# Third and fourth Strassen sums in a buffer of their own, nine Strassen operand pairs, 205 Strassen steps at other places

## The chip, the cores and the metric

The kernel runs on one core of one Trainium2 chip. The metric is the device time of one execution in microseconds, the median of several runs. Beside it there is one profiled execution, whose trace gives what each engine did.

## The reference

A decoder block over 256 tokens of 4096 channels, in float32. Cut to what matters:

```python
h = rmsnorm(x, norm_w)
proj = einsum('bsd,de->bse', h, w_in)            # 4096 -> 20480
u_p, z_p, u_c, b_c, c_c, z_c, g_logit = split(proj)
y_pool = causal_multiscale_pool(u_p, pool_w[l], pool_scale) * silu(z_p)
y_conv = causal_gated_shortconv(u_c, b_c, c_c, conv_w, conv_b) * silu(z_c)
br = einsum('bsnc,ncd->bsnd', stack([y_pool, y_conv]), w_branch)   # 2 x (2048 -> 4096)
merged = sum(sigmoid(g_logit + gate_b) * br, axis=n)
x = x + einsum('bsd,de->bse', merged, w_out)     # 4096 -> 4096
return rmsnorm(x, final_norm_w)
```

## The kernel before

**Units and steps.** The three large products are cut into units of 1024 output columns: 20 of the input projection (cu, cc, cz, cb for the two halves of the convolution branch, pz and pu for the two halves of the pooling branch, then eight gate units g0_0, g1_0, ... g1_3), eight of the branch projection (b0_0, b1_0, ...), four of the output projection (o0 to o3). They run in the order given here. A unit sums over steps; one step brings 256 rows of the weights (two blocks of 128 rows by 1024 columns, 1 MB) and multiplies them with one *operand pair*, the matching 256 channels of all 256 tokens, which stay in SBUF in a tile named `arena`. A unit of the input or output projection has 16 steps, one for each operand pair; a branch unit has eight. In two units (pz1 and g0_0) three more steps, for the pooling, stand among the first.

**Precision.** Each float32 factor is cut into a high part (ScalarE copies it to the matmul type `F32R`) and a low part (VectorE subtracts the high part from the original), and a product is three matmuls: high by high, high by low, low by high.

**P steps and S steps.** A plain step (P) is 2 token halves x 2 column halves x 2 row blocks x 3 = 24 matmuls of 128x512. A Strassen step (S) takes seven block products for eight, 7 x 3 = 21 matmuls, and pays for it in sums: of the operand pair once (the blocks called Q3, Q5, Q6, Q7 in the arena), and of the weights in every S step. `Step.micros` lists what a step prepares. For a P step these are two halves, each with a copy by ScalarE and a subtraction by VectorE of 128x1024. For an S step: `sums` adds the first two sums, 128x1024, into `V`; `direct` copies and subtracts three raw blocks (128x1536), and adds the third and the fourth sum (128x512 each) into `raw` itself, over blocks 0 and 1; `t13` splits V; `t24` splits the third and fourth sum. All results go to `ring`, a ring buffer of 60 pieces of 1 KB per partition. A P step takes 16 pieces, an S step 28.

**What sets the order.** Every engine runs its instructions in program order, and the order is written by the planner at build time. `pump` issues the next weight load (SyncE's queue, three `raw` buffers of 1 MB) once the step three before is *prepared*, and prepares a step up to AHEAD = 3 steps before its matmuls, as soon as the ring has room. `tick` runs once in every 6 matmuls: it takes the next item of `queue` (a unit's epilogue: its joins, sigmoid, products, transposes, stores) and advances the filling of the operand pairs of the next projection (`pop_fill`: a sum set and a split). The large adds between units and the transfers of intermediate results are issued on GpSimd's queue.

**Operand pairs.** Of the 16 pairs NP_X = 9 have plain slots and NS_X = 7 have Strassen slots. An S step needs a pair with a Strassen slot; a P step can use either kind. One of the seven slots (NB = 1) has two blocks more, so that its plain and its Strassen form stand side by side. Because some units have eight S steps, one plain pair (`LATE`) gets its sums separately: `late_sums` makes them at step 23 and stores them in DRAM, `early_place` and `late_split` fetch and split them for later units, and `late_m` does the same in o1. The sums of the other pairs are made by `x_sums` and split by `x_parts` at the steps that `seconds` lists.

**Which steps are S steps.** Each unit has a sequence of P and S, made by `spread_sequence`, `late_sequence`, `at_places` and the table `SPREAD`. In all there are 188 S steps and 260 P steps.

Of the kernel before, what the change touches and what calls it, by code (L numbers as in the profile page):

```python
# [42 lines left out]
NP_X, NS_X = 9, 7  # L43
NB = 1
NP_Y, NS_Y = (6, 5), (2, 3)
RING = 60
# [10 lines left out]
def hybrid_block(ctx: ExitStack, tc: tile.TileContext, x, x_t, norm_t, w_first, w_in, pool_w, pool_scale,  # L57
# [52 lines left out]
    V = sb("V", [P, 2, NH])  # L110
    cnt = sb("cnt", [P, 2])
# [16 lines left out]
    late_d = dram.tile([P, 5, P], F32, name="late_d")  # L128
# [62 lines left out]
    class Operand:  # L191


        def __init__(self, kind, view, region):
            self.kind, self.view, self.region = kind, view, region
            self.ready = False
            self.more = None
            self.more_ready = False

        def block(self, part, i):  # L200

            if self.kind == "S":
                return self.view[:, part, i]
            if i in self.more:
                return self.more[i][:, part]
            return self.view[:, part, {A12: 0, A22: 0, A11: 1, A21: 1}[i], i in (A22, A21)]
# [40 lines left out]
    class Step:  # L247
# [7 lines left out]
        def micros(self):  # L255
# [30 lines left out]
            if self.kind == "S":  # L286
                q = r.rearrange("p (i n) -> p i n", i=4)
                tv = V

                def sums(_):  # L290
                    add(tv, q[:, 0:1].to_broadcast([P, 2, NH]), q[:, 1:3])

                def direct(block):
                    self.bd = block
                    d = piece(block, 0, 12).rearrange("p (i a n) -> p i a n", i=3, a=2)
                    self.dh, self.dl = d[:, :, 0], d[:, :, 1]
                    act(self.dh, q[:, 1:4])
                    add(q[:, 0], tv[:, 0], q[:, 2])
                    sub(self.dl, q[:, 1:4], self.dh.bitcast(F32))
                    add(q[:, 1], q[:, 0], q[:, 3])  # L300

                def t13(block):
                    self.b13 = block
                    t = piece(block, 0, 8).rearrange("p (i a n) -> p i a n", i=2, a=2)
                    self.h13, self.l13 = t[:, :, 0], t[:, :, 1]
                    act(self.h13, tv)
                    sub(self.l13, tv, self.h13.bitcast(F32))
# [297 lines left out]
    SPREAD = {"cc1":(8,1),"cb1":(8,2),"cu1":{4,5,7,9,10,12,13,15},"cb0":(8,2),"cz0":(7,5),"pz0":{5,7,8,10,11,13,15},"pu0":(7,),"cz1":(7,5),"g1_3":(6,0),"pz1":(7,),"g0_0":(7,),"pu1":{4,6,8,10,12,13,15},"cc0":{2,4,6,8,10,13,15}}  # L605
# [26 lines left out]
    def in_unit(name, col, epi, seq=None, **kw):  # L632
        def src(i):
            return win[col // NU, i]
        if name in SPREAD:
            at = SPREAD[name]
            seq = at_places(at) if isinstance(at, set) else spread_sequence(*at)
# [5 lines left out]
        units.append(Unit(name, src, seq or seq_late, x_ops, epi, scaled=True, **kw))  # L643
        return units[-1]


    def conv_units(c, first=False):
# [32 lines left out]
        in_unit(f"cu{c}", base, lambda u: [], seq=seq_0 if first else spread_sequence(NS_X, 4), dst=Y)  # L680
        in_unit(f"cc{c}", base + 2 * HALF, c_epi, seq=seq_even if c else None)
        in_unit(f"cz{c}", base + 3 * HALF, z_epi)
        in_unit(f"cb{c}", base + HALF, b_epi, seq=seq_even)


    def pool_units(c):
        def z_epi(u):
            return sigmoid_mul() + [
                lambda: move(E[:, 0], pool_scale[0, None, c * NU:(c + 1) * NU].to_broadcast([P, NU]))
            ] + gap(5) + [lambda: mul(Y, R, E[:, 0:1].to_broadcast([P, 2, NU]))]  # L690

        in_unit(f"pz{c}", HALF + c * NU, z_epi, seq=None if c else seq_turned)
        in_unit(f"pu{c}", c * NU, lambda u: [])
        return units[-1]


    def make_bands(c):
        nonlocal sa, Y
        if c == 0:
            x_ops[LATE].more_ready = False  # L700

# [78 lines left out]
    def gate_unit(n, c, before=None):  # L780
# [7 lines left out]
        seq = {(0, 0): seq_late, (1, 3): spread_sequence(few)}.get((n, c), seq_even)  # L788
        if (n, c) in ((0,1),(1,1),(0,2),(1,2),(0,3),(1,0),):
            seq = spread_sequence(NS_X + 1, 1 if c else 2)  # L790
# [27 lines left out]

    def out_unit(c):
# [14 lines left out]
        seq = seq_even if c else seq_late  # L834
        if c in (2,):
            seq = spread_sequence(NS_X + 1)
        if c == 1:
            seq = at_places({2,4,6,7,9,11,13,15})

            late_s = [i for k, i in seq if k == 'S']  # L840
            late_s = iter(late_s[1:] + late_s[:1])
            seq = [(k, next(late_s) if k == 'S' else i) for k, i in seq]
        if c == 3:

            seq = spread_sequence(NS_X, 1, TAIL + 0)
        if c == 2:
            seq = at_places({2,4,6,7,9,11,13,15})
# [133 lines left out]
    def insert(u, c, owner):  # L981
# [144 lines left out]
    LATE = NP_X - 1  # L1126

    def late_sums():
        o = x_ops[LATE]
        h, l = (o.view[:, part].bitcast(F32) for part in range(2))  # L1130
        q = sa[:, 4:8].rearrange("p (k t) c -> p k t c", t=2)
        add(q, h, l)
        q = q.rearrange("p k t c -> p k (t c)")
        mul(q, q, rbc[:, None].to_broadcast([P, 2, T]))
        sums_s(sa, [sa[:, i] for i in range(4, 8)])
        mul(sa[:, Q3], sa[:, Q3], std)
        move(late_d[:, 0:4], sa[:, 0:4])
        move(late_d[:, 4], sa[:, A11])

    def late_place(pool, o, blocks):  # L1140
        n = len(blocks)
        q = pool.tile([P, 2, n, P], F32R, name="sums")
        o.more = {b: q[:, :, i] for i, b in enumerate(blocks)}
        return q

    def late_split(o, place, src):

        q = []
        return [lambda: (q.append(place()), act(q[0][:, 0], src)),
                lambda: (sub(q[0][:, 1], src, q[0][:, 0].bitcast(F32)), setattr(o, "more_ready", True))]  # L1150

    early = []

    def early_place():

        pool = replace_by("early")
        src = pool.tile([P, 5, P], F32, name="early_src")
        move(src, late_d)
        early.extend(late_split(x_ops[LATE], lambda: late_place(pool, x_ops[LATE], (Q3, Q5, Q6, Q7, A11)), src))

    late = []

    def late_m():
        nonlocal Y
        pool = replace_by("late_m", lower)
        stages.pop()
        Y = pool.tile([P, 1, NU], F32, name="Y")
        sums_s(sa, [sa[:, i] for i in range(4, 8)])
        late.append(late_place(pool, m_ops[LATE], (Q3, Q5, Q6, Q7)))

# [12 lines left out]
    seconds = {14: 10, 15: 11, 16: 12, 17: 13, 19: 14, 21: 15, 28: 9}  # L1183
# [50 lines left out]
    def pump():  # L1234

        while True:
            moved = False
            nl = state["nl"]
            if nl < len(loaded) and (nl < NRAW or loaded[nl - NRAW].prepared):
# [7 lines left out]
            if i < len(steps) and i <= state["limit"]:  # L1247
                s = steps[i]
                if s.src is None or s.raw is not None:
# [10 lines left out]
                    if not state["micros"]:  # L1260
                        s.prepared = True
# [6 lines left out]
    for s in steps:  # L1268
        s.prepared = False
# [36 lines left out]
    def queue_fills():  # L1306
# [26 lines left out]
        for i in order_of(seq_late):  # L1333
            from_m(m_ops[i], i)

    def run_step(u, st):
# [14 lines left out]
        assert st.kind != "S" or st.op.kind == "S" or st.op.more_ready  # L1351
# [11 lines left out]
    for u in units:  # L1363
# [11 lines left out]
        for st in u.steps:  # L1375
# [11 lines left out]
            if u.name == "g0_0" and st is u.steps[2]:  # L1387
                move(sa[:, 0:5], late_d)
            if u.name == "g0_0" and st is u.steps[8]:
                queue.extend(late_split(x_ops[LATE], lambda: late_place(  # L1390
                    replace_by("late", lower), x_ops[LATE], (Q3, Q5, Q6, Q7, A11)), sa[:, 0:5]))
            if u.name == "o1" and st is u.steps[4]:
                assert not fills
                move(flat(sa[:, 4:8]), m_d[LATE // 4][:, LATE % 4].rearrange("p k t -> p (k t)"))
                queue.extend(gap(7) + [late_m] + late_split(m_ops[LATE], lambda: late[0], sa[:, 0:4]))
# [179 lines left out]
```

## Time and profile before

| | |
|---|---|
| median of 3 runs | 2378.28 us (2378.14 to 2378.44) |
| span of the profiled execution, first to last instruction | 2376.6 us |
| time of the runs outside that span | about 1.7 us |
| PE busy | 2364.3 us (99%), 10540 instructions |
| DVE busy | 2170.1 us (91%) |
| ACT busy | 1392.8 us (59%) |
| POOL busy | 86.0 us (4%) |
| HBM read and written | 516.60 MB and 25.49 MB |
| granted TensorE clock | 0.999 |

PE is TensorE, PEld its weight loads, DVE VectorE, ACT ScalarE, POOL GpSimd, SP SyncE. A line such as L1283 is a line of the kernel's file; most elementwise work goes through one helper, so that it has one line (L72 for VectorE's two-tensor operations, L69 for ScalarE) and is told apart by its tiles. In `ring<-raw,ring` the tile left of the arrow is written, those right of it are read. The records of matmuls overlap, so their mean (390 ns) is not their pace.

### The profile page before, as it was taken

How to read it: one execution, taken by the hardware profiler on the slowest of the kernel's cores; microseconds unless marked ns; L12 is line 12 of the kernel's file. 1: busy time of each engine (PE TensorE's matmuls, PEld its weight loads, DVE VectorE, ACT ScalarE, POOL GpSimd, SP SyncE). 2: the span in 40 equal slices, each digit the busy share in tenths (PEclk: the TensorE clock that was granted, in tenths of full speed). 3: DMA queues.
4: the chain of work that ended last, by engine and by line, in shares of the span. 5: the costliest groups of instructions: out<-in, count | busy, mean ns of one | idle time of the engine just before them, and what ended most of it. 6: DMA issues, size and time to landing. Idle time of an engine off the chain costs nothing.

```text
span 2376.6 us, 27878 instructions
## 1 busy us (share of the span) xinstructions
PE 2364.3 (99%) x10540; PEld 1957.5 (82%) x10540; DVE 2170.1 (91%) x2195; ACT 1392.8 (59%) x1452; POOL 86.0 (4%) x153
## 2 busy tenths in 40 slices
PE   9999999999999999999999999999999999999998
PEld 7888888888888888888888888888888888888886
DVE  8999999989989978979999999999898898799998
ACT  7565665656546555556655656556664556566554
POOL 0000000000010010000000000000100001000000
PEclk9999999999999999999999999999999999999999
DMA  8464665655665646655776667667766667567666
GB/s 337 161 238 170 235 251 211 217 211 213 212 239 217 238 183 221 231 200 201 259 247 214 235 237 235 228 238 260 263 249 230 226 250 289 209 214 265 241 240 264
DMA packets 83559, 551.25 MB, mean 232 GB/s; under 512 B 9616, under 2 KB 9872, under 8 KB 22240
## 3 DMA queue, kind: packets, MB, share of 16 engines
q1 hardware_dynamic: 68800, 484.51, 54.7%
q0 software_dynamic: 14192, 63.90, 9.6%
q8 instruction: 82, 1.34, 0.2%
q10 hardware_dynamic: 432, 1.07, 0.1%
q14 instruction: 53, 0.43, 0.1%
HBM read 516.60 MB, written 25.49 MB: 228 GB/s over the span
## 4 chain that ended last, share of the span: by engine, by line
PE 98%; DVE 1%; DMA 1%; ACT 0%; SPq 0%; issue 0%; DVEq 0%; ACTq 0%
PE sums L1283 74%; PE shared L1283 21%; PE shared L766 1%; PE shared L509 1%; DMA raw<-in_w_in_dram 0%; DVE R L72 0%; DVE ring L72 0%; DMA raw<-in_w_out_dram 0%; ACT ring L69 0%; PE shared L745 0%; SPq L87 0%; PE shared L746 0%; PE shared L748 0%; SPq L162 0%; ACT V L69 0%
## 5 line engine op out<-in xcount | busy, mean ns | idle before, releaser
L1283 PE MATMUL sums<-ring,arena 128*128 128x512 f32 x7890 | 1858.2, 390 | 0.5 <-ACT arena L69 0.4
L1283 PEld LDWEIGHTS sums<-ring,arena 128*128 128x128 f32 x7890 | 1478.3, 188 | 307.8 <-ACT ring L69 1.2
L69 ACT ACTIVATE ring<-raw 128x1024 fp32r<-128x1024 f32 (+2 forms) x902 | 997.5, 1145 | 703.9 <-DVE raw L72 297.3
L72 DVE TENSOR_TENSOR ring<-raw,ring 128x1024 fp32r<-128x1024 f32 (+2 forms) x902 | 1176.5, 1335 | 142.5 <-ACT ring L69 108.6
L1283 PE MATMUL shared<-ring,arena 128*128 128x512 f32 x2118 | 535.2, 389 | 0.0
L1283 PEld LDWEIGHTS shared<-ring,arena 128*128 128x128 f32 x2118 | 397.6, 188 | 82.5
L69 ACT ACTIVATE ring<-V 128x1024 fp32r<-128x1024 f32 x188 | 198.8, 1058 | 148.3 <-DVE V L72 112.7
L72 DVE TENSOR_TENSOR V<-raw 128x1024 f32<-128x1024 f32 x188 | 229.3, 1220 | 4.7 <-DMA raw<-in_w_in_dram 2.6
L72 DVE TENSOR_TENSOR ring<-V,ring 128x1024 fp32r<-128x1024 f32 x188 | 229.3, 1220 | 0.5 <-ACT ring L69 0.5
L72 DVE TENSOR_TENSOR raw<-raw 128x512 f32<-128x512 f32 x188 | 130.2, 693 | 6.5
L72 DVE TENSOR_TENSOR raw<-V,raw 128x512 f32<-128x512 f32 x188 | 130.0, 692 | 5.8
L72 DVE TENSOR_TENSOR R<-R,E 128x1024 f32<-128x1024 f32 (+1 forms) x49 | 77.5, 1591 | 1.6 <-ACT E L69 0.9
L72 DVE TENSOR_TENSOR R<-R,shared 128x512 f32<-128x512 f32 x87 | 59.5, 684 | 8.9 <-ACT R L69 5.0
L69 ACT ACTIVATE E<-sums,rin 128x512 f32<-128x512 f32 x76 | 50.0, 685 | 15.7 <-PE sums L1283 15.7
L69 ACT ACTIVATE arena<-sa 128x512 fp32r<-128x512 f32 (+2 forms) x42 | 22.4, 559 | 35.5 <-DVE sa L72 35.5
L1283 PE MATMUL shared<-ring,sums 128*128 128x512 f32 x138 | 35.9, 396 | 0.0
L1283 PEld LDWEIGHTS shared<-ring,sums 128*128 128x128 f32 x138 | 25.9, 188 | 6.0
L94 POOL DMA_DIRECT2D R<-E x8 | 7.2, 980 | 513.6 <-ACT ring L69 337.9
L69 ACT ACTIVATE E<-sums 128x512 f32<-128x512 f32 x40 | 22.2, 592 | 5.4 <-PE sums L1283 5.1
L72 DVE TENSOR_TENSOR arena<-sa,arena 128x512 fp32r<-128x512 f32 (+2 forms) x42 | 24.4, 606 | 0.7 <-ACT arena L69 0.7
L94 POOL DMA_DIRECT2D R<-in_gate_b_dram x9 | 10.1, 1119 | 356.0 <-DVE R L72 348.3
L509 PEld LDWEIGHTS shared<-ident,R 128*128 128x128 f32 x160 | 19.4, 140 | 4.2
(149 smaller groups left out, 515.8 us busy)
## 6 DMA issues: line engine op xcount, KB each, us to landing
raw<-in_w_in_dram SPq DMA_DIRECT2D x318, 1024.0 KB, 4.9
raw<-in_w_branch_dram SPq DMA_DIRECT2D x64, 1024.0 KB, 5.4
raw<-in_w_out_dram SPq DMA_DIRECT2D x64, 1024.0 KB, 5.0
gates_d<-R POOLq DMA_DIRECT2D x8, 1024.0 KB, 9.1
R<-in_gate_b_dram POOLq DMA_DIRECT2D x7, 1024.0 KB, 11.2
R<-E POOLq DMA_DIRECT2D x4, 1024.0 KB, 8.7
raw<-in_pool_w_dram SPq DMA_DIRECT2D x4, 1024.0 KB, 5.0
Y<-gates_d POOLq DMA_DIRECT2D x4, 1024.0 KB, 7.9
```

The costliest lines, as they stand in the source:

```text
L69: return pin(nc.scalar.activation(dst, src, func, **kw))
L72: return pin(nc.vector.tensor_tensor(out=dst, in0=a, in1=b, op=op))
L94: return pin(nc.gpsimd.dma_start(dst, src, accum_op=ALU.add))
L509: pin(nc.tensor.transpose(shared(j)[:, i * T + t * P:i * T + (t + 1) * P], src[:, t, c:c + P], ident))
L766: pin(nc.tensor.matmul(o, a[:, k, ts], b[:, k], start=(k, i) == (0, 0), stop=(k, i) == (3, 2)))
L1283: pin(nc.tensor.matmul(ps, lhs, rhs, start=n == 0, stop=n == u.total[b] - 1))
```

## The change

It does these things:

- A new tile `W` of the size of V takes the third and the fourth sum, which were written over the raw weights.
- A step has a second mark, `split`, set when `direct` is done (for a P step, when it is prepared). `pump` issues the load three steps on by that mark and no longer by `prepared`.
- Nine pairs have Strassen slots and seven have plain ones; two of the nine (NB = 2) have the two blocks more. The functions for the late pair are gone, with their DRAM tile and their transfers; `seconds` makes the sums of pairs 8 and 7 at steps 32 and 36.
- The order of P and S steps comes from a table of places for each unit, 205 S steps and 243 P steps in all. Units with nine S steps appear. `insert` puts several S steps between two P steps in pz1 and g0_0.
- The ring has 62 pieces. The scratch that is set aside for descriptors of GpSimd's transfers is set to 2048 bytes per partition.

```diff
-NP_X, NS_X = 9, 7
-NB = 1
+NP_X, NS_X = 7, 9
+NB = 2
...
-RING = 60
+RING = 62
...
+    W = sb("W", [P, 2, NH])
...
-                    add(q[:, 0], tv[:, 0], q[:, 2])
+                    add(W[:, 0], V[:, 0], q[:, 2])
                     sub(self.dl, q[:, 1:4], self.dh.bitcast(F32))
-                    add(q[:, 1], q[:, 0], q[:, 3])
+                    add(W[:, 1], W[:, 0], q[:, 3])
+                    self.split = True
...
-                    act(self.h24, q[:, 0:2])
-                    sub(self.l24, q[:, 0:2], self.h24.bitcast(F32))
+                    act(self.h24, W)
+                    sub(self.l24, W, self.h24.bitcast(F32))
...
+    PLACES = {
+        "cc0": (2, 4, 6, 7, 10, 12, 15),
+        "cz0": (5, 7, 8, 10, 11, 13, 15),
+        "cb0": (1, 3, 5, 6, 8, 11, 12, 14, 15),
+        "cu1": (4, 5, 7, 9, 10, 11, 12, 14, 15),
+        "cc1": (3, 5, 6, 8, 9, 11, 12, 14, 15),
...
+        "pz1": (3, 6, 8, 9, 10, 11, 12, 14, 15),
+        "pu1": (4, 5, 6, 9, 10, 12, 13, 15),
+        "g0_0": (3, 6, 8, 9, 10, 12, 14, 15),
+        "g1_0": (2, 4, 5, 7, 8, 9, 11, 13, 15),
+        "g0_1": (2, 4, 6, 7, 8, 10, 11, 13, 15),
...
+    }
...
+    OUT = ((6, 7, 9, 10, 11, 13, 15), (2, 4, 6, 7, 8, 10, 12, 13, 15), (2, 4, 6, 9, 11, 13, 15), (1, 3, 4, 7, 9, 10, 12))
...
-        while ssteps:
-            seq.append(ssteps.pop(0))
-            if rest:
-                seq.append(rest.pop(0))
+        n = len(ssteps) // (len(rest) + 1)
+        while ssteps:
+            seq += ssteps[:n] + rest[:1]
+            ssteps, rest = ssteps[n:], rest[1:]
...
-    seconds = {14: 10, 15: 11, 16: 12, 17: 13, 19: 14, 21: 15, 28: 9}
+    seconds = {14: 10, 15: 11, 16: 12, 17: 13, 19: 14, 21: 15, 28: 9, 32: 8, 36: 7}
...
-    before(23, late_sums)
-    before(40, early_place)
-    before(41, lambda: early[0]())
-    before(42, lambda: early[1]())
...
-            if nl < len(loaded) and (nl < NRAW or loaded[nl - NRAW].prepared):
+            if nl < len(loaded) and (nl < NRAW or loaded[nl - NRAW].split):
...
-    nc = _bacc.Bacc("TRN2", target_bir_lowering=False, num_devices=1)
+    nc = _bacc.Bacc("TRN2", target_bir_lowering=False, num_devices=1,
+                     dynamic_dma_scratch_size=2048)
```

S steps by unit, before and after: cb0 8 and 9, cu1 8 and 9, cc1 8 and 9, cz1 7 and 8, pz0 7 and 8, pu0 7 and 8, pz1 7 and 9, pu1 7 and 8, g0_0 7 and 8, g1_0 8 and 9, g0_1 8 and 9, g0_2, g1_2 and g0_3 8 and 9 each, g1_3 6 and 7, o0 6 and 7, o1 8 and 9, o2 8 and 7; the others keep their number (cu0 0, cc0 and cz0 7, cb1 and g1_1 8, o3 7, the branch units 2, 3 or 0). The order within o0 was PPPPPSPSPSPSPSPS and becomes PPPPPPSSPSSSPSPS, counted from step 0.

More of the change, by code (lines that the diff above doesn't have):

```diff
@@ L196, in __init__ @@
             self.ready = False
-            self.more = None
-            self.more_ready = False
         def block(self, part, i):
[L202 to L206, printed above, removed]
+            return self.view[:, part, i]
     busy = {}
@@ L287, in micros @@
                 q = r.rearrange("p (i n) -> p i n", i=4)
-                tv = V
                 def sums(_):
-                    add(tv, q[:, 0:1].to_broadcast([P, 2, NH]), q[:, 1:3])
+                    add(V, q[:, 0:1].to_broadcast([P, 2, NH]), q[:, 1:3])
                 def direct(block):
@@ L305, in t13 @@
                     self.h13, self.l13 = t[:, :, 0], t[:, :, 1]
-                    act(self.h13, tv)
-                    sub(self.l13, tv, self.h13.bitcast(F32))
+                    act(self.h13, V)
+                    sub(self.l13, V, self.h13.bitcast(F32))
                 def t24(block):
@@ L604, in hybrid_block @@
     LAST_FIRST = ('cc0',)
-    SPREAD = {"cc1":(8,1),"cb1":(8,2),"cu1":{4,5,7,9,10,12,13,15},"cb0":(8,2),"cz0":(7,5),"pz0":{5,7,8,10,11,13,15},"pu0":(7,),"cz1":(7,5),"g1_3":(6,0),"pz1":(7,),"g0_0":(7,),"pu1":{4,6,8,10,12,13,15},"cc0":{2,4,6,8,10,13,15}}
+    PLACES = {
[19 rows of a table added]
+    }
+    GATE = (2, 4, 5, 7, 8, 10, 11, 13, 15)
     def late_sequence(ns_):
@@ L634, in src @@
             return win[col // NU, i]
-        if name in SPREAD:
-            at = SPREAD[name]
-            seq = at_places(at) if isinstance(at, set) else spread_sequence(*at)
+        if seq is None:
+            seq = at_places(PLACES[name])
             if name in LAST_FIRST:
@@ L642, in in_unit @@
                 seq = [(k, next(pairs_s) if k == 'S' else i) for k, i in seq]
-        units.append(Unit(name, src, seq or seq_late, x_ops, epi, scaled=True, **kw))
+        units.append(Unit(name, src, seq, x_ops, epi, scaled=True, **kw))
         return units[-1]
@@ L678, in b_epi @@
                 lambda: put(y_d[1, c], chan(Y))]
-        in_unit(f"cu{c}", base, lambda u: [], seq=seq_0 if first else spread_sequence(NS_X, 4), dst=Y)
-        in_unit(f"cc{c}", base + 2 * HALF, c_epi, seq=seq_even if c else None)
+        in_unit(f"cu{c}", base, lambda u: [], seq=seq_0 if first else None, dst=Y)
+        in_unit(f"cc{c}", base + 2 * HALF, c_epi)
         in_unit(f"cz{c}", base + 3 * HALF, z_epi)
-        in_unit(f"cb{c}", base + HALF, b_epi, seq=seq_even)
+        in_unit(f"cb{c}", base + HALF, b_epi)
     def pool_units(c):
@@ L699, in make_bands @@
         if c == 0:
-            x_ops[LATE].more_ready = False
             close(upper)
@@ L786, in epi @@
                 lambda: act(R, R, AF.Sigmoid), lambda: move(gates_d[n, c], R)]
-        seq = {(0, 0): seq_late, (1, 3): spread_sequence(few)}.get((n, c), seq_even)
-        if (n, c) in ((0,1),(1,1),(0,2),(1,2),(0,3),(1,0),):
-            seq = spread_sequence(NS_X + 1, 1 if c else 2)
+        seq = None
         u = in_unit(f"g{n}_{c}", 6 * HALF + n * D + c * NU, epi, seq=seq, before=start)
@@ L833, in src @@
             return wout[c, i]
[L834 to L847, printed above, removed]
+        seq = at_places(OUT[c])
         units.append(Unit(f"o{c}", src, seq, m_ops, epi, before=start))
@@ L1123, in x_parts @@
             sub(o.view[:, 1, a:b], sa[:, a:b], o.view[:, 0, a:b].bitcast(F32))
[L1126 to L1169, printed above, removed]
     def before(i, fn, *args):
@@ L1260, in pump @@
                     if not state["micros"]:
-                        s.prepared = True
+                        s.prepared = s.split = True
                         state["micros"] = None
@@ L1268, in hybrid_block @@
     for s in steps:
-        s.prepared = False
+        s.prepared = s.split = False
     def tick():
@@ L1332, in queue_fills @@
                 from_y(n, y_last[n][i], i, lambda: all(o.ready for q in y_ops for o in q))
-        for i in order_of(seq_late):
+        for i in order_of(at_places(OUT[0])):
             from_m(m_ops[i], i)
@@ L1350, in run_step @@
             pop_fill(True)
-        assert st.kind != "S" or st.op.kind == "S" or st.op.more_ready
+        assert st.kind != "S" or st.op.kind == "S"
         gs = st.groups()
@@ L1386, in hybrid_block @@
                 queue_fills()
[L1387 to L1395, printed above, removed]
             if u.before and st is u.steps[len(u.steps) * 3 // 4]:
```

3 lines of the change are left out of this document (1 added, 2 removed), and 9 rows, old and new, of the table PLACES.

## The prediction

> **What bounds the kernel now.** I read the page first, then who waited for whom on PE, then the chain of waits, then DVE in order of time.
>
> ```profile
> span 2376.6 us, 27878 instructions
> ...
> PE 2364.3 (99%) x10540; PEld 1957.5 (82%) x10540; DVE 2170.1 (91%) x2195; ACT 1392.8 (59%) x1452; POOL 86.0 (4%) x153
> ...
> PE 98%; DVE 1%; DMA 1%; ACT 0%; SPq 0%; issue 0%; DVEq 0%; ACTq 0%
> ```
> ```profile
> PE shared L1034 <- DVE rout L1039: 1.1, 1, 1.1
> PE sums L1283 <- ACT arena L69: 0.4, 1, 0.4
> ```
> ```profile
> 1991.87 66.64 PE sums L1283 x294
> ```
>
> PE is 98% of the chain that ended last, and these are all its waits: 1.5 us in the whole execution. So the time is the number of matmuls times their pace. The chain gives the pace without the overlap that the busy columns hold: 66.64 / 294 = 0.2267 us. A P step has 24 matmuls, 5.44 us; an S step has 21, 4.76 us. DVE is second at 91%; whether it stays second decides this change. Its price per step is read from start to start, since a record reaches into the next one:
>
> ```profile
> 1307.14 2.35 DVE L72 TENSOR_TENSOR ring<-raw,ring 128x1024 fp32r<-128x1024 f32 x2
> 1309.41 1.22 DVE L72 TENSOR_TENSOR V<-raw 128x1024 f32<-128x1024 f32 x1
> 1310.67 0.69 DVE L72 TENSOR_TENSOR raw<-V,raw 128x512 f32<-128x512 f32 x1
> 1311.28 1.75 DVE L72 TENSOR_TENSOR ring<-raw,ring 128x1536 fp32r<-128x1536 f32 x1
> 1313.07 0.69 DVE L72 TENSOR_TENSOR raw<-raw 128x512 f32<-128x512 f32 x1
> 1313.67 1.22 DVE L72 TENSOR_TENSOR ring<-V,ring 128x1024 fp32r<-128x1024 f32 x1
> 1314.94 1.23 DVE L72 TENSOR_TENSOR ring<-raw,ring 128x1024 fp32r<-128x1024 f32 x1
> 1316.09 1.22 DVE L72 TENSOR_TENSOR V<-raw 128x1024 f32<-128x1024 f32 x1
> ```
>
> A P step (first row) takes DVE 1309.41 - 1307.14 = 2.27 us, an S step (the next six) 1316.09 - 1309.41 = 6.68 us. So against PE an S step loses 6.68 - 4.76 = 1.92 us of DVE's lead, and a P step wins 5.44 - 2.27 = 3.17 us.
>
> **The change part by part.** *17 more S steps* (205 for 188; the built program has 10,485 matmuls for 10,536). PE: 17 x 3 x 0.2267 = 11.56 us less, all on the path. The Trainium skill ("TensorE: Matmul & The Clock Gate", Part 1, the section on the measured gap) puts a warm 512-column matmul at 215.7 ns; by it the gain would be 11.0 us. The trace's 226.7 ns for this operand type decides.
>
> *W beside the raw weights.* Before, the second small add overwrites what the 1536-wide subtraction reads, and starts only after it (1311.28 + 1.75 = 1313.03, start 1313.07). Where nothing is waited for, the next start lies 0.08 us before the record's end (1310.67 + 0.69 = 1311.36, start 1311.28). After, this add reads W and raw and waits for the first W add alone, one instruction further back. I take 0.12 us less for each of 205 S steps, 6.56 us each; the ends are 0 and 0.12. It reaches the time only through DVE's lead. Raw is also freed two subtractions earlier, which moves each load behind an S step earlier on SP's queue; PE waited for no load here, so nothing is gained, and an earlier load cannot be late. W adds one wait: the next S step's first add into W stands behind ACT's copy of the old W, with the whole DVE queue behind it. DVE's own subtraction of that W waited for the same copy just before, so it costs nothing.
>
> *DVE by unit.* Busy time before, in the units that get tightest (the second conv unit cu1, the gate unit g1_0, a plain gate unit g0_1, and the output units o0 and o1):
>
> ```profile
> 342.19:425.79 83.60, 83.60 (x378) 69.16 (x377) 81.35 (x76) 48.03 (x47) 2.01 (x3) 1.00 0.62 225
> 1119.83:1201.57 81.74, 81.74 (x361) 67.59 (x360) 78.37 (x74) 49.86 (x48) 4.09 (x5) 1.00 0.75 253
> 1201.57:1283.32 81.75, 81.75 (x362) 67.59 (x360) 75.78 (x71) 48.49 (x48) 1.80 (x2) 1.00 0.68 232
> 2035.23:2119.98 84.75, 84.75 (x384) 70.35 (x382) 76.83 (x95) 49.52 (x62) 0.53 (x1) 1.00 0.54 196
> 2119.98:2201.68 81.70, 81.70 (x362) 67.57 (x360) 79.10 (x78) 50.76 (x52) 5.15 (x7) 1.00 0.77 264
> ```
>
> The columns are the stretch, its length, and busy PE, PEld, DVE, ACT and POOL; so in g0_1, the third row, DVE is busy for 75.78 of 81.75 us. One S more adds 6.68 - 2.27 = 4.41 and takes 0.68 from PE: 80.19 of 81.07, and with nine S steps at 0.12 less 79.1. So a nine-S gate unit fits, with 2 us over. cu1 comes to 85.76 - 1.08 = 84.7 for 82.9; its 1.8 us too much are covered by cb0 before it and cc1 after it. g1_0 and o1 lose the late split too. I cost them at 0, from 0 to 1 us each.
>
> *Two more sets of sums* (pairs 8 and 7, at steps 32 and 36, in cz0), in place of the late ones of pair 8:
>
> ```profile
> 147.81 0.75 DVE L72 TENSOR_TENSOR sa<-arena 128x256 f32<-128x256 f32 x2
> ...
> 150.38 0.29 DVE L72 TENSOR_TENSOR sa<-sa,std 128x128 f32<-128x128 f32 x1
> ...
> 152.86 0.88 DVE L72 TENSOR_TENSOR arena<-sa,arena 128x512 fp32r<-128x512 f32 x2
> ```
>
> One set is (150.67 - 147.81) + 0.88 = 3.7 us of DVE, so 7.4 us are added while the old late sums (about 2.9, the same five rows) and their split go. cz0 opens with five P steps, which win 5 x 3.17 = 15.9 us; I cost it at 0, at most 1 us.
>
> *o0, where I expect a wait.* Its places go from every second step to S S P S S S (steps 6 to 11), and there DVE also fills the last four operands. Their price, and what ACT held up in the same stretch:
>
> ```profile
> 2061.63 0.28 DVE L72 TENSOR_TENSOR sa<-Y 128x128 f32<-128x128 f32 x1
> ...
> 2062.56 0.69 DVE L72 TENSOR_TENSOR raw<-V,raw 128x512 f32<-128x512 f32 x1
> ...
> 2070.12 0.69 DVE L72 TENSOR_TENSOR arena<-sa,arena 128x512 fp32r<-128x512 f32 x1
> 2070.73 0.62 DVE L72 TENSOR_TENSOR arena<-Y,arena 128x256 fp32r<-128x256 f32 x2
> 2071.26 2.35 DVE L72 TENSOR_TENSOR ring<-raw,ring 128x1024 fp32r<-128x1024 f32 x2
> ...
> 2076.38 0.69 DVE L72 TENSOR_TENSOR arena<-sa,arena 128x512 fp32r<-128x512 f32 x1 [0.70 <-ACT arena L69]
> ...
> 2086.26 1.23 DVE L72 TENSOR_TENSOR ring<-raw,ring 128x1024 fp32r<-128x1024 f32 x1 [1.02 <-ACT ring L69]
> ```
>
> A fill's sums take 2062.56 - 2061.63 = 0.93 us, its split 2071.26 - 2070.12 = 1.14 us. Count from o0's start, with 84.75 - 10 x 5.44 - 6 x 4.76 = 1.79 us of transposes ahead of its 16 steps. PE reaches step 6 at 1.79 + 6 x 5.44 = 34.4, then steps 7, 8, 9, 10, 11 at 39.2, 44.0, 49.4, 54.2, 58.9. The ring (62 pieces; 16 for a P step, 28 for an S step) lets the last block of step 7 be written only when step 5 is consumed, at 34.4; with ACT's copy ahead of DVE's subtraction (each about 1.2, the second from the row 1313.67) it is ready at 36.8. From there DVE works without a pause: step 8 and one sum 2.27 + 0.93, ready 40.0; step 9 and a split 6.56 + 1.14, 47.7; step 10 with two sums and a split 6.56 + 3.00, 57.3. That is 3.1 behind PE's arrival, and just in time, because the last block is needed 16 matmuls in (3.6 us). Step 11's first block needs V, an add and the wide subtraction: 57.3 + 1.26 + 0.61 + 1.67 = 60.8, where PE's second matmul wants it at 58.9 + 0.2 = 59.1: PE waits 1.7 us. Its last block is ready at 60.8 + 0.61 + 1.14 + 1.27 + 1.15 = 65.0 (an add, the last split, two subtractions), where PE, shifted, needs it at 58.9 + 1.7 + 3.6 = 64.2: 0.8 us more. Sum 2.5 us; with the 0.70 and 1.02 us of ACT's hold-ups it is 4.2. I take 3.0.
>
> *The rest.* Ring 62 for 60 and the removed late moves on POOL cost nothing: POOL is 4% busy. The end of the kernel (o3 keeps seven S steps and three P steps at the tail) stays as it is.
>
> Sum: 2376.6 - 11.56 + 3.0 = 2368.0 us of span. The median of the runs, 2378.28, lies 1.7 us above the span; I keep that: 2369.7 us.
>
> **The rivals.** *DVE keeps up everywhere* (o0's fills fall elsewhere): 2378.28 - 11.56 = 2366.7. For it: DVE before falls behind nowhere. Against: the sum for o0. Chance 0.22.
>
> *DVE becomes the bound.* If W saves nothing, cu1, g1_0 and o1 are over by 81.35 + 4.41 - 82.92 = 2.8, 78.37 + 4.41 - 81.06 = 1.7 and 79.10 + 4.41 - 81.02 = 2.5 us, and three S steps in a row cost 5.8 us of lead in many units. 2369.7 + 7.0 = 2376.7. Against it: the neighbours have 3 us to spare. Chance 0.13.
>
> *The clock falls in o0.* After the last matmul the granted clock does not hold:
>
> ```profile
> 2366.10:2376.60 10.50, 0.00 (x0) 0.00 (x0) 4.28 (x14) 2.46 (x6) 0.00 (x0) 0.66 0.72 282
> ```
>
> A mean of 0.66 in 10.5 us without a matmul is full clock for the first 3.4 us if it then is half. If o0's 4.2 us came as one gap, some 3.4 us at half clock would follow and cost 1.7: 2366.7 + 4.2 + 1.7 = 2372.6. The waits summed above are two, of 1.7 and 0.8, so it should not. Chance 0.04. The Trainium skill (the same page and part) says that an idle window of about 3.4 us halves the clock; the row agrees.
>
> *POOL's transfers queue up: slower.* With 2048 bytes of scratch for POOL's transfers, one that must wait for the one before to drain lands a landing later.
>
> ```profile
> R<-E POOLq DMA_DIRECT2D x4, 1024.0 KB, 8.7
> ```
> ```profile
> q0 software_dynamic: 14192, 63.90, 9.6%
> ```
>
> The kernel leaves 9 ticks of 6 matmuls, 12.2 us, for this landing of 8.7. Twice 8.7 is 17.4, so DVE would stand 5.2 us behind its add; the lead of some 4 us that it has in a unit's opening P steps leaves 1.2 us, in 20 units 24 us: 2369.7 + 24 = 2393.7. It decides once two such transfers do not fit. Against it: POOL's own queue (q0) takes 9.6% of the DMA engines' span. Chance 0.08. The Trainium skill ("DMA: Bandwidth & Descriptors", "The descriptor swizzle" and "Terms") has nine 16-byte descriptors a side and engine for 1 MiB; my estimate from it is that 2048 bytes hold 128, a dozen such transfers. No run here shows it.
>
> *The change not doing what it says* can be left out: the built program has the 51 matmuls less.
>
> **How the numbers follow.** My forecast has 0.53. 0.2% is 4.8 us, about what a measurement of this kernel tells from no change, so faster means under 2373.5: forecast, first rival and clock rival, 0.79. Within: most of the DVE rival, 0.12. Slower: POOL's, and a DVE rival that goes further, 0.09. The range runs from the floor, 2366.5, to 2376.7 with the DVE rival; beyond lies about 0.1.
>
> **What would show it.** Right: about 51 matmuls fewer at 0.2267 us; the add into W starting before the wide subtraction's record ends; PE's waits on DVE ring in o0 alone, 2 to 4 us, the longest under 2 us; DVE at 94 to 96%. Wrong: PE waits for DVE ring in cu1, g1_0 or o1; DVE waiting for a POOL landing (E or R); a clock under 1.00 within the span.

## The result, and the profile after

| | before | after |
|---|---|---|
| median | 2378.47 us (2378.02 to 2379.36, 20 runs) | 2374.04 us (2372.42 to 2378.09, 20 runs) |
| span of the profiled execution | 2376.6 us | 2373.2 us |
| its own run time | 2378.28 us | 2374.87 us |

After is faster by 4.4 us: ratio 0.9984, interval 0.9977 to 0.9990. The forecast was 2369.7 us, in a range from 2366.5 to 2376.7: the sign is right, the time lies in the range, and the point is 4.3 us too low. The runs of after lie 5.7 us apart, those of before 1.3 us; the experiments show some of what makes the difference.

The page of after:

```profile
span 2373.2 us, 27863 instructions
...
PE 2355.6 (99%) x10489; PEld 1947.1 (82%) x10489; DVE 2224.4 (94%) x2279; ACT 1418.4 (60%) x1472; POOL 87.6 (4%) x148
...
PE 93%; DVE 4%; ACT 1%; issue 1%; DMA 1%; SPq 0%; DVEq 0%; ACTq 0%
```

51 matmuls fewer, as intended, and DVE up from 91% to 94%. But PE's share of the chain that ended last has fallen from 98% to 93%: at some places the end of the kernel now hangs on DVE. Who waited for whom on PE (us in total, times, the longest):

```profile
PE sums L1233 <- ACT E L69: 2.5, 2, 2.3
PE sums L1233 <- DVE ring L72: 1.9, 4, 0.8
PE shared L1033 <- DVE rout L1038: 1.1, 1, 1.1
PE shared L1233 <- DVE ring L72: 1.1, 2, 0.6
PE sums L1233 <- ACT ring L69: 0.3, 1, 0.3
```

Only the third line stood there before. The others have these places in the order of time on PE (start, busy time, and in brackets the idle time before it):

```profile
751.73 0.74 PE L1233 MATMUL sums<-ring,arena 128*128 128x512 f32 x2 [0.54 <-DVE ring L72]
...
930.88 1.43 PE L1233 MATMUL sums<-ring,arena 128*128 128x512 f32 x5 [0.49 <-DVE ring L72]
932.66 0.51 PE L1233 MATMUL sums<-ring,arena 128*128 128x512 f32 x1 [0.34 <-ACT ring L69]
933.92 0.73 PE L1233 MATMUL sums<-ring,arena 128*128 128x512 f32 x2 [0.75 <-DVE ring L72]
...
1731.39 3.92 PE L1233 MATMUL sums<-ring,arena 128*128 128x512 f32 x16 [2.29 <-ACT E L69]
...
2090.24 0.39 PE L1233 MATMUL shared<-ring,arena 128*128 128x512 f32 x1
2091.23 0.74 PE L1233 MATMUL shared<-ring,arena 128*128 128x512 f32 x2 [0.60 <-DVE ring L72]
...
2093.21 0.39 PE L1233 MATMUL shared<-ring,arena 128*128 128x512 f32 x1
2094.11 2.12 PE L1233 MATMUL shared<-ring,arena 128*128 128x512 f32 x8 [0.51 <-DVE ring L72]
```

These are the last S step of pz0, the last of pz1, the opening of b1_0, and step 11 of o0. Only the last is the place that the prediction named. Since records of matmuls overlap, a wait in brackets is short of what it costs. I measure the loss from start to start: what the multiplications of a unit take beyond 0.2267 us for each. Over all units that is 6.6 us before and 15.1 us after. The units that changed most: b1_0 +2.59, pz1 +2.46, o0 +1.74, pz0 +0.87, pu0 +0.65, b0_0 +0.49. So the span should move by -11.56 + 8.5 = -3.1 us; it moved by -3.4.

### The profile page after: what moved, and what is told of

It is laid out like the page before. It is cut to its first block, busy times and chain, and to the rows that moved or that the text cites. A ratio compares the mean times of both kernels' runs of the same rounds, so it can differ in the third digit from the quotient of the medians.

```text
span 2373.2 us, 27863 instructions
## 1 busy us (share of the span) xinstructions
PE 2355.6 (99%) x10489; PEld 1947.1 (82%) x10489; DVE 2224.4 (94%) x2279; ACT 1418.4 (60%) x1472; POOL 87.6 (4%) x148
## 4 chain that ended last, share of the span: by engine, by line
PE 93%; DVE 4%; ACT 1%; issue 1%; DMA 1%; SPq 0%; DVEq 0%; ACTq 0%
PE sums L1233 69%; PE shared L1233 22%; DVE ring L72 2%; PE shared L778 1%; ACT ring L69 1%; PE shared L503 1%; DVE W L72 1%; DVE V L72 1%; DMA raw<-in_w_in_dram 0%; DVE arena L72 0%; DMA raw<-in_w_branch_dram 0%; DVE sa L72 0%; PE shared L757 0%; SPq L87 0%; DVE R L72 0%
## 5 line engine op out<-in xcount | busy, mean ns | idle before, releaser
L1233 PE MATMUL sums<-ring,arena 128*128 128x512 f32 x7671 | 1813.9, 390 | 4.8 <-ACT E L69 2.5
L1233 PEld LDWEIGHTS sums<-ring,arena 128*128 128x128 f32 x7671 | 1436.9, 188 | 305.9 <-DVE ring L72 3.8
L72 DVE TENSOR_TENSOR ring<-raw,ring 128x1024 fp32r<-128x1024 f32 (+2 forms) x697 | 941.2, 1380 | 75.4 <-ACT ring L69 73.1
L69 ACT ACTIVATE ring<-raw 128x1024 fp32r<-128x1024 f32 (+2 forms) x697 | 799.8, 1180 | 241.5 <-PE sums L1233 137.7
L1233 PE MATMUL shared<-ring,arena 128*128 128x512 f32 x2460 | 621.5, 389 | 1.3 <-DVE ring L72 1.1
L1233 PEld LDWEIGHTS shared<-ring,arena 128*128 128x128 f32 x2460 | 461.2, 188 | 99.2 <-DVE ring L72 3.6
L69 ACT ACTIVATE ring<-W 128x1024 fp32r<-128x1024 f32 x205 | 217.8, 1063 | 360.1 <-DVE W L72 314.5
L72 DVE TENSOR_TENSOR ring<-W,ring 128x1024 fp32r<-128x1024 f32 x205 | 251.2, 1225 | 13.9 <-ACT ring L69 2.2
L72 DVE TENSOR_TENSOR W<-V,raw 128x512 f32<-128x512 f32 x205 | 141.7, 691 | 6.4
L72 DVE TENSOR_TENSOR W<-W,raw 128x512 f32<-128x512 f32 x205 | 140.5, 686 | 0.0
```

Source lines behind the costliest of these rows:

```text
L69: return pin(nc.scalar.activation(dst, src, func, **kw))
L72: return pin(nc.vector.tensor_tensor(out=dst, in0=a, in1=b, op=op))
L1233: pin(nc.tensor.matmul(ps, lhs, rhs, start=n == 0, stop=n == u.total[b] - 1))
```

## The experiments

The kernel after is taken as the base, unless said otherwise. Medians are from as many runs as are named, and ratios are to the kernel before.

**After once more.** 

> The changed kernel itself once more, to see whether its waits stand at the same places and why its runs spread over 5.7 us (2372.4 to 2378.1) where those of before spread over 1.3. Theory (VectorE's order is late in pz0, pu0, pz1 and o0, and ScalarE's queue behind it in b1_0): 2372 to 2376 us, waits of PE again at the ends of pz0 and pz1, at step 11 of o0 and at the opening of b1_0, together 6 to 10 us. Rival (the waits come from chance arrivals of loads): the same total, but at other places.

Measured: 2375.5 us (2371.48 to 2378.13, 11 runs), ratio 0.9987 (0.9978 to 0.9995), span 2373.4 us. The same kernel thus gave medians of 2374.04 and 2375.5 us: a smaller difference between two medians below shows nothing by itself, and what an edit did is read from its trace. The waits in pz0, pz1 and o0 stand at the same places with the same sizes to 0.1 us. The opening of b1_0 does not: it cost 4.17 us for 2.59. The waiting itself was the same, but the clock (the column after the busy times, 0.76 and 0.75) fell behind it:

```profile
1729.00:1732.00 3.00, 2.02 (x6) 1.64 (x7) 3.00 (x5) 3.00 (x6) 0.00 (x0) 0.76 0.89 328
1732.00:1736.00 4.00, 4.00 (x14) 3.17 (x14) 3.97 (x5) 2.65 (x3) 0.54 (x1) 0.75 0.89 317
```

(0.24 x 3 + 0.25 x 4) / 0.5 = 3.4 us at half clock; eight matmuls took 0.20 us more each, 1.6 us in all. In the profile of after these stretches have 1.00. The loss of pu0, 0.65 us in after, is not there at all.

**W undone**: the two sums again over the raw weights, at after's 205 places. With them goes the mark `split`, and so the earlier load; the next experiment but one takes away the earlier load alone.

```diff
-                    add(W[:, 0], V[:, 0], q[:, 2])
+                    add(q[:, 0], V[:, 0], q[:, 2])
                     sub(self.dl, q[:, 1:4], self.dh.bitcast(F32))
-                    add(W[:, 1], W[:, 0], q[:, 3])
-                    self.split = True
+                    add(q[:, 1], q[:, 0], q[:, 3])
...
-                    act(self.h24, W)
-                    sub(self.l24, W, self.h24.bitcast(F32))
+                    act(self.h24, q[:, 0:2])
+                    sub(self.l24, q[:, 0:2], self.h24.bitcast(F32))
```

> The third and fourth sum go over the raw weights again and the next load waits for the whole step; all else, W's memory too, stays. Theory: an S step takes VectorE 6.67 us for 6.54, as in the trace before, 27 us over 205 S steps; where VectorE has its lead used up (pz0 to pu1, g0_2 to b0_0, o0) each unit with 8 or 9 S steps loses up to 1.1 us more: 8 to 14 us slower than the changed kernel, 2382 to 2388. Rival (W saves nothing): 2374, within 1 us of the changed kernel.

Measured: 2400.19 us (2397.95 to 2402.85, 4 runs), ratio 1.0092 (1.0078 to 1.0105), span 2397.4 us. W is worth 25 us here, about twice what I expected. The three largest of PE's waits in its profile:

```profile
PE shared L1232 <- DVE ring L72: 8.2, 10, 2.1
PE sums L1232 <- DVE ring L72: 7.0, 10, 1.1
PE sums L1232 <- ACT E L69: 2.7, 3, 2.1
```

Twenty waits for the ring in place of six, in some 15 units; g1_3 alone lost 8.5 us, with one wait that cost 2.25 us from start to start and was followed by eight matmuls at half clock. DVE's S step takes 6.67 us, from one V to the next:

```profile
1306.64 1.22 DVE L72 TENSOR_TENSOR V<-raw 128x1024 f32<-128x1024 f32 x1
...
1313.31 1.22 DVE L72 TENSOR_TENSOR V<-raw 128x1024 f32<-128x1024 f32 x1
```

**W alone in the kernel before**, with its 188 S steps at their old places: the same sums and splits the other way round, without `split`, and with the scratch of 2048 bytes.

> W alone, put into the kernel before with its 188 S steps at their old places (and the scratch of 2048 bytes, which makes room for W). VectorE's S step gets shorter by 0.12 us 188 times, 22.6 us of its time. Theory (W pays only through VectorE's lead, and before the change the lead was never used up): the time is that of before, 2378.1 to 2378.5 us, with the same 1.5 us of PE waits. Rival (VectorE's time is on the path everywhere, so that W is worth its 22.6 us in any order of steps): 2356 to 2360 us.

Measured: 2378.3 us (2377.9 to 2378.57, 11 runs), ratio 0.9999 (0.9990 to 1.0008), span 2376.8 us. Its page and its only two waits on PE:

```profile
PE 2365.0 (100%) x10540; PEld 1958.2 (82%) x10540; DVE 2153.9 (91%) x2195; ACT 1394.2 (59%) x1452; POOL 86.3 (4%) x153
```
```profile
PE shared L1035 <- DVE rout L1040: 1.1, 1, 1.1
PE sums L1284 <- DVE ring L72: 0.2, 1, 0.2
```

DVE is busy for 16.2 us less (2170.1 before) and the time stays. So the same edit is worth nothing with 188 S steps at the old places and 25 us with 205 at the new ones. W is no gain by itself; it pays for the S steps.

**The earlier load undone**: `pump` goes by `prepared` again.

```diff
-            if nl < len(loaded) and (nl < NRAW or loaded[nl - NRAW].split):
+            if nl < len(loaded) and (nl < NRAW or loaded[nl - NRAW].prepared):
```

> Only the mark that releases the load goes back to prepared; W stays. The load behind an S step is issued some 2.4 us of VectorE's work later. Theory (loads land in 4.8 us while VectorE needs over 9 us for the next two steps): within 1 us of the changed kernel, 2373 to 2375. Rival (the earlier load is what keeps VectorE going between S steps in a row): 2378 or more, with more idle time of VectorE behind loads than the 10 us of the changed kernel.

Measured: 2374.53 us (2372.39 to 2376.15, 11 runs), ratio 0.9983 (0.9974 to 0.9992). No difference from after that its two medians don't have too, as predicted.

**The small scratch alone, in the kernel before**: `dynamic_dma_scratch_size=2048`.

> The kernel before with the scratch of 2048 bytes and nothing else. Theory: POOL's transfers do not queue up, 2378.3 within 0.5 us, landing of R<-E 8.6 to 8.8 us. Rival (a transfer waits for the one before): up to 24 us slower, landings near double.

Measured: 2378.51 us (2378.03 to 2379.1, 11 runs), ratio 1.0000 (0.9991 to 1.0009), landing of R<-E 8.8 us. In the kernel before the small scratch costs nothing; in after it was not tried by itself.

**pz1 with eight S steps** (204 in all).

```diff
-        "pz1": (3, 6, 8, 9, 10, 11, 12, 14, 15),
+        "pz1": (3, 6, 8, 9, 10, 12, 14, 15),
```

The table only says which pairs take the S form in pz1; `insert` sets the order. Nine S steps with two P steps left over become S S S P S S S P S S S at the unit's end; eight with three become S S P S S P S S P S S.

> pz1 with eight S steps for nine (S S P S S P S S P S S in place of S S S P S S S P S S S after its first steps); 204 S steps in all. Theory (runs of three S steps use VectorE's lead up, so that PE waits 2.4 us at pz1's last step): the waits in pz1 go, three matmuls (0.68 us) come: 1.7 us less than the changed kernel's 2374 to 2375, about 2373. Rival (VectorE is short in the whole stretch pz0 to g0_0): the wait only moves into pu1, and the time rises by 0 to 0.7 us.

Measured: 2372.65 us (2370.53 to 2374.72, 8 runs), ratio 0.9975 (0.9965 to 0.9985). What pz1 loses falls from 3.0 to 0.54 us, what it was before the change. One S step fewer costs 0.7 us of matmuls and saves 2.5 us of waiting; the rival's wait in pu1 did not come. In DVE's order of time in after, the last three S steps in pz1:

```profile
914.08 1.22 DVE L72 TENSOR_TENSOR V<-raw 128x1024 f32<-128x1024 f32 x1
...
915.94 1.75 DVE L72 TENSOR_TENSOR ring<-raw,ring 128x1536 fp32r<-128x1536 f32 x1
917.61 0.68 DVE L72 TENSOR_TENSOR W<-W,raw 128x512 f32<-128x512 f32 x1
...
920.64 1.22 DVE L72 TENSOR_TENSOR V<-raw 128x1024 f32<-128x1024 f32 x1
...
927.22 1.22 DVE L72 TENSOR_TENSOR V<-raw 128x1024 f32<-128x1024 f32 x1
...
933.78 2.35 DVE L72 TENSOR_TENSOR ring<-raw,ring 128x1024 fp32r<-128x1024 f32 x2
```

Three S steps take DVE 933.78 - 914.08 = 19.7 us, and PE 3 x 4.76 = 14.3. Three such runs with one P step between two of them spend 9 x 1.8 and win 2 x 3.17: the lead is gone at the last step, where PE waits three times.

**No fill work in the last two steps of b0_0.**

```diff
-        pop_fill()
+        if not state["hold"]:
+            pop_fill()
...
+            state["hold"] = u.name == "b0_0" and st in u.steps[-2:]
             run_step(u, st)
```

> In the last two steps of b0_0 no filling of operands is advanced, so that ScalarE's queue has no copy of sa ahead of the copies that empty b0_0's sums banks; all 205 S steps stay. Theory (ScalarE stands 2.7 us behind VectorE's sums, the evacuation behind that, and PE 2.4 us behind the evacuation, after which the clock falls in some executions): the wait at b1_0's opening goes, 2.4 to 4.2 us less, about 2371, and the spread of the runs falls below 3 us. Rival (the evacuation is late because the last S step of b0_0 itself is): the wait stays, 2374 to 2375.

Measured: 2371.22 us (2370.2 to 2375.09, 9 runs), ratio 0.9973 (0.9963 to 0.9983), span 2369.5 us. The wait at b1_0's opening is gone (under 0.2 us). The runs were expected to spread by less than 3 us and spread by 4.9: two of the nine took 2374.89 and 2375.09 us, so b1_0's opening is not the only thing that varies. ACT in after, around that opening (in brackets the idle time before an instruction):

```profile
1724.15 1.05 ACT L69 ACTIVATE ring<-raw 128x1024 fp32r<-128x1024 f32 x1
1727.92 1.04 ACT L69 ACTIVATE arena<-sa 128x512 fp32r<-128x512 f32 x2 [2.72 <-DVE sa L72]
1728.88 1.99 ACT L69 ACTIVATE ring<-raw 128x1024 fp32r<-128x1024 f32 x2
1730.77 1.55 ACT L69 ACTIVATE E<-sums 128x512 f32<-128x512 f32 x3
```

and with the fills held back:

```profile
1723.08 2.95 ACT L69 ACTIVATE ring<-raw 128x1024 fp32r<-128x1024 f32 x3
1725.92 1.56 ACT L69 ACTIVATE E<-sums 128x512 f32<-128x512 f32 x3
```

b1_0 starts on banks that ACT empties into E. ACT works in program order, and there the split of a fill (`arena<-sa`) stands ahead of those copies; the fill's sums come from DVE, which in after stands behind. So ACT idles for 2.72 us with PE's banks full, although ACT is busy for only 60% of the span. ACT's own work is not slow: DVE's delay goes on to ACT, and from it to PE.

DVE's delay has an origin that the traces show. In b0_0 DVE stood still for a transfer on GpSimd's queue, the gate bias, which is issued at 1692.70 and lets DVE go on at 1707.99, 15.3 us later. The two views are GpSimd's and DVE's in order of time, in after:

```profile
1692.70 1.23 POOL L94 DMA_DIRECT2D R<-in_gate_b_dram  x1 [1.44 <-DVE R L72]
```
```profile
1707.99 2.36 DVE L72 TENSOR_TENSOR R<-R,E 128x1024 f32<-128x1024 f32 x2 [2.42 <-DMA R<-in_gate_b_dram]
```

In the kernel before DVE came to this add 22.9 us after the issue (1688.65 and 1711.50) and waited for nothing. In six profiles that are alike up to here but for small edits, b1_0's loss follows this wait (in us):

| | DVE waits for the landing | b1_0 loses |
|---|---|---|
| after | 2.42 | 2.59 |
| after once more | 2.37 | 4.17, of it 1.6 by the clock |
| bands' operations later | 2.38 | 2.60 |
| pz1 with eight | 1.53 | 1.71 |
| o0 spread | 1.30 | 1.51 |
| earlier load undone | 1.03 | 1.21 |

Each time the loss is some 0.2 us more than the wait. With the fills held back DVE waited 2.44 us for the landing, and PE lost nothing. Why the transfer lands later than before was not tried.

**The bands' small operations three steps later.**

```diff
-    before(141+2, end_bands, 0)
+    before(141+5, end_bands, 0)
```

> The 2 us of small VectorE work that make the pooling bands move from the last S step of pz0 to the third step of pu0, a P step. Theory: the wait of 0.8 us at pz0's last step goes and the 0.3 us in pu0 too: 0.8 to 1.1 us less. Rival (VectorE's work is only moved, and its lead is as short behind as before): the wait reappears in pu0, no change.

Measured: 2373.3 us (2372.2 to 2375.84, 11 runs), ratio 0.9980 (0.9971 to 0.9988). pz0's loss falls from 1.33 to 0.46 us, its size of before. In after, `end_bands` puts 745.03 - 743.07 = 2.0 us of ten small operations ahead of pz0's last S step:

```profile
743.07 0.28 DVE L743 TENSOR_REDUCE cnt<-sa 128x1 f32<-128x128 f32 x1
...
745.03 1.22 DVE L72 TENSOR_TENSOR V<-raw 128x1024 f32<-128x1024 f32 x1
```

The median is 0.7 us under after's, less than after's two medians differ by; it is the trace that shows the gain. pu0 loses 0.56 us here, 0.64 in after and nothing in its repeat, so whether the 0.3 us expected there went can't be told. In this profile the openings of b0_0 and b1_0 cost 2.5 and 2.6 us: they change from one execution to the next.

**o0's S steps spread.**

```diff
-    OUT = ((6, 7, 9, 10, 11, 13, 15), ...
+    OUT = ((5, 7, 9, 11, 13, 14, 15), ...
```

> o0's seven S steps at 5, 7, 9, 11, 13, 14, 15 in place of 6, 7, 9, 10, 11, 13, 15, so that the four late fills meet S steps with a P step between them. Theory: the two waits in o0's step 11 (1.4 us) go; up to 0.7 us come back at the opening of o1, since three S steps now end o0: 0.7 to 1.5 us less. Rival (the four fills alone use up the lead): a wait of over 1 us at o0's step 13 or 15.

Measured: 2375.29 us (2372.99 to 2377.3, 11 runs), ratio 0.9986 (0.9978 to 0.9995). The expected gain did not come. The wait at step 11 is gone, and a larger one stands at step 15, behind three S steps in a row; o0 loses 2.94 us for 1.93. PE there:

```profile
2109.39 1.43 PE L1233 MATMUL sums<-ring,arena 128*128 128x512 f32 x5 [0.78 <-DVE ring L72]
2111.16 0.50 PE L1233 MATMUL sums<-ring,arena 128*128 128x512 f32 x1 [0.35 <-ACT ring L69]
2112.43 0.73 PE L1233 MATMUL sums<-ring,arena 128*128 128x512 f32 x2 [0.76 <-DVE ring L72]
```

The theory was that the run of S steps among the fills is to blame; the rival, that o0's lead is too small for seven S steps and the fills wherever they stand, fits what came.

**The three helpful edits together**, with pz1's S step given to o2, so that it is 205 again.

```diff
-... (2, 4, 6, 9, 11, 13, 15), (1, 3, 4, 7, 9, 10, 12))
+... (2, 4, 6, 7, 9, 11, 13, 15), (1, 3, 4, 7, 9, 10, 12))
```

> The three small edits together (pz1 with eight S steps, end_bands three steps later, no fill pieces in b0_0's last two steps); the S step taken from pz1 is given to o2, so that 205 stay. Theory (the time is 205 S steps' matmuls plus the separate waits, and each wait stands by itself): pz1's excess falls by 2.46, b1_0's by 2.6, pz0's by 0.87, nothing comes back: 2374.0 - 5.9 = 2368.1 us, PE waiting only in o0 step 11 (1.43) and by less than 0.7 elsewhere. Rival (the lead that one wait gave DVE or ACT was needed later, so a wait removed comes back at the next tight place, the openings of b0_0 and b1_0 or g1_3): 2370 to 2372 us, with 2 to 3 us of waits for ACT E or DVE ring at those places.

Measured: 2368.13 us (2367.86 to 2369.79, 5 runs), ratio 0.9956 (0.9942 to 0.9970): the forecast sum, and 5.9 us faster than after. That it fits to 0.1 us is in part chance, since after's two medians differ by 1.5. The runs lie 1.9 us apart. PE's waits in its profiled execution, which is the slowest of the five runs (2369.79 us):

```profile
PE sums L1234 <- ACT E L69: 1.7, 2, 1.3
PE shared L1234 <- DVE ring L72: 1.1, 2, 0.6
PE shared L1033 <- DVE rout L1038: 1.1, 1, 1.1
PE sums L1234 <- ACT ring L69: 0.5, 1, 0.5
```

Left are o0's step 11 and, in this execution, the opening of b0_0 (2.3 us). The rival named this opening; but it costs 2.5 us with the bands' operations alone moved, and nothing in after's repeat. ACT holds PE up here too, but what it waits for is a load of weights: its splits (`ring<-raw`) stand ahead of the copies that empty the banks.

```profile
1680.33 2.01 ACT L69 ACTIVATE ring<-raw 128x1024 fp32r<-128x1024 f32 x2 [2.51 <-DMA raw<-in_w_branch_dram]
```

ACT waited 2.5 to 3.0 us for this load here, with the bands moved and with pz1 at eight, where b0_0 lost 2.3, 2.5 and 1.7 us; it waited 0.8 to 2.2 us in six other profiles with the new places, where b0_0 lost 0.5 us or nothing. So the rival of the repeat, chance arrivals of loads, fits this opening.

**The same with o0 at (6, 7, 9, 10, 12, 13, 15).**

> As the kernel with three edits, and in o0 the S step of place 11 goes to place 12 (places 6, 7, 9, 10, 12, 13, 15), so that no three S steps stand together there. Theory (o0's wait comes from three S steps in a row with fill work between them): the 1.43 us at step 11 go, 2366.7 us. Rival (o0 has too little lead for seven S steps and the fills wherever they stand): the wait moves to step 13 or 15 at 1 to 2.5 us, 2368 to 2369 us.

Measured: 2368.81 us (2368.31 to 2370.45, 5 runs), ratio 0.9960 (0.9946 to 0.9974). The wait moves to step 13, in one piece of 1.64 us, and o0 loses 2.29 us in all: the rival again.

## Why the prediction was right, and where it was wrong

The forecast took 3.0 us of new losses off 11.56 us of gain, all of them in o0. The losses were 8.5 us, 1.7 of them in o0; the other 6.8 us had no term. That the time still lies in the range is in part luck: its upper end came from the rival that W saves nothing, and W saves a lot.

**The 11.56 us on PE.** Right: 51 matmuls fewer. That the pace held is seen in the kernel with the three edits: with most waits gone, 205 S steps come to 2368.13 us, 1.4 us above the 2366.7 that the count of matmuls alone gave.

**W's 0.12 us.** Right in size and in reason: 6.56 and 6.58 us from V to V in pz1 (920.64 - 914.08, 927.22 - 920.64), for 6.67 with W undone, and the add into W starts 917.69 - 917.61 = 0.08 us before the wide subtraction's record ends. That it reaches the time only through DVE's lead was right too: 0 us with 188 S steps, 25 with 205.

**The price of W's absence.** Wrong. The rival "DVE becomes the bound" took 7.0 us if W saved nothing, from cu1, g1_0 and o1. It cost 25. That this is near DVE's whole 205 x 0.12 = 24.6 us is not shown to be more than coincidence: g1_0, g0_2 and o1 lost nothing with nine S steps each, and g1_3 lost 8.5 us with seven (0.8 us of DVE's time), 1.6 of it by the clock. The unit totals found three units too tight; PE waited in some 15.

**o0.** The place was right to the step: two waits, at step 11's second matmul and at its last block. The size was 1.74 us for the 3.0 taken; at the two matmuls themselves 2091.23 - 2090.24 - 0.23 = 0.76 and 2094.11 - 2093.21 - 0.23 = 0.67 us (from the start of the record ahead of each) for the 1.7 and 0.8 summed. DVE went through the steps without a pause, in the order counted, and came a microsecond earlier: V of step 11 starts 2087.56 - 2031.33 = 56.2 us after o0's start for the 57.3 counted.

```profile
2087.56 1.22 DVE L72 TENSOR_TENSOR V<-raw 128x1024 f32<-128x1024 f32 x1
```

ACT held nothing up from step 8 on, for which I had raised 2.5 to 3.0. The term was mis-sized, not misplaced.

**The step that failed: "DVE by unit".** I summed DVE's work over five units and took a unit that fits, or that its neighbours cover, as free. The five cost 0.1 us or less each, o0's named wait aside, as said. But the sum does not see the order within a unit, nor units that I left out. pz1 (+2.46) ends on three runs of three S steps; pz0 (+0.87) has 2 us of small operations ahead of its last S step; both waits went in the trace of an experiment that takes only that away. pu0 (+0.65) is not in after's repeat. The statement that PE would wait for DVE's ring in o0 alone was wrong with it.

**What the prediction gave no price: a landing, and ACT behind it.** b1_0's opening cost 2.6 us, and 4.2 us in the repeat, through an engine with 40% idle time. The prediction looked at ACT only where it holds up DVE. Here DVE's delay reached PE by an in-order instruction on ACT that stands ahead of the one PE needs, and DVE's delay was a wait for a landing on GpSimd's queue. That is a sign of being wrong that the prediction named, "DVE waiting for a POOL landing (E or R)": 2.4 us for R in b0_0 and 1.2 us for E in pz0. The prediction counted on the landing of R<-E, 8.7 us, and on a queue that takes 9.6% of the DMA engines' span; this one transfer took 15.3 us. Whether the small scratch has a part in it is open: the kernel before waits for neither, and W alone in it, with the same scratch, waits 2.5 us for E and not for R.

**The clock.** It was put at 0.04, and in o0. Between the first and the last matmul it did not fall in the profile of after, but in its repeat it did, at b1_0, and cost 1.6 us more. The waiting with and without that fall, together with the openings' own variation (b1_0 by 1.4 us without the clock, b0_0 by 2.5), fits the spread of after's runs, and the spread shrinks to 1.9 us where the three edits took most waits away. That every slow execution of after is one of these is argued, not shown.

**The rest.** The two additional sets of sums in cz0 and the earlier load: 0, as costed. The ring of 62 was not tried by itself. DVE at 94%: right.

## What to carry to other kernels

When a change trades the bound engine's work for the second engine's, count the second engine's lead step by step through every stage, with runs of expensive steps and small housekeeping at their places; totals by stage don't show where it runs out. Saved time on the second engine was worth nothing here while there was lead, and 25 us once there was little, so try such an edit together with the work that it pays for. And where lead is short, look on the third engine for in-order instructions that wait for the second, or for a load, ahead of those the first needs; follow such a wait back to where it began, here to a landing.

## What was not expected of the hardware

The granted clock fell to half for 3.4 us after PE had waited for only 2.4 us (b1_0 in the repeat) and 2.25 us (g1_3 with W undone), but not after 2.46 us at the same place in after. The prediction expected it only from one gap of the size of 3.4 us.

The clock's records in these traces show what differs. From its first rise on the clock changes only at points that lie whole multiples of 3.413 us apart: in the repeat it is full for 1723.73 us (505 of them), half for one, and full for 631.47 us (185). The two waits behind which it fell lie whole between two such points: PE idles from 1727.74 to 1729.98 in the repeat and the clock falls at 1730.58; it idles from 1696.68 to 1698.77 in g1_3 and the clock falls at 1699.00. In after a point at 1730.00 cuts the idle time of 2.29 us into 0.90 and 1.39, and the clock holds; so it does for 2.27 us with the bands moved (1.13 and 1.14) and for 2.10 us in b1_0 with W undone (0.83 and 1.27). So in these runs 2.09 us of idle time between two points was enough and 1.64 us, the longest that left the clock alone, was not; whether a wait falls whole between two points changes from one execution to the next.

The Trainium skill ("TensorE: Matmul & The Clock Gate", Part 1, "What's actually happening") speaks of an idle window of about 3.4 us that runs freely; the 3.4 us at half clock and the spacing of the points agree with its length, and the runs here show that a shorter wait can be enough, in some executions.
